# Hyena filters: last layer, decay and spectra issued behind the first tiles of the input projection, and GpSimd's arithmetic of that stage given to VectorE

## The chip, the core and the metric

The kernel runs on one core of a Trainium2 chip. The core has TensorE (matrix products, written to PSUM), VectorE and ScalarE (elementwise work; ScalarE also evaluates functions), GpSimd (elementwise work, without PSUM) and SyncE, from which this kernel issues nearly all of its transfers. Each engine runs its own instructions in order and waits on semaphores of the others. The profile calls them PE (and PEld for its weight loads), DVE, ACT, POOL and SP. The metric is the device time of one execution in microseconds, the median of several.

## The reference, cut to what matters

A diffusion trunk of two layers, on 512 latent and 128 context tokens. Layer 0 mixes with an mLSTM and with a Hyena long convolution, behind one input projection. What the change touches:

```python
hp = rmsnorm(x, g_mix) * (1.0 + sc) + sh        # sc, sh = two of the six columns of silu(c) @ w_ada + b
proj = h @ w_in                                 # 28 column tiles of 128, 12 of them for Hyena
v_h, x1, x2 = split(dwconv3(hy, w_conv_hy))
u = x1 * v_h

def hyena_filters(L, w1, b1, w2, b2, w3, freq):
    hdn = sin(fr * (z @ w1 + b1))
    hdn = sin(fr * (hdn @ w2 + b2))
    filt = hdn @ w3                             # 64 -> 1024
    filt = filt * exp(-t * deltas)              # the decay
    return filt[:, :512], filt[:, 512:]         # h_past, h_future

y_h = x2 * (long_conv_bidir(u, h_past, h_future) + hy_bias * u)   # by spectra of u and of the filters
```

## The kernel before, in words

All tokens lie side by side in 640 columns, with the 1024 features in 8 blocks (k) of 128 partitions. A product in full precision is made of three fp32r matmuls: each operand is split into a high and a low part (`XH`, `XL` for the activations, `hya0h`, `hya0l` and so on for a weight tile), and high*high, high*low and low*high are added in PSUM. ScalarE makes the high part of a weight (L102), another engine the low part (L103, `split_w`).

The start of the program, in `mixer_ab`, is this:

- `hyena_filters` is a generator that the caller steps with `next(filt)`, so that its pieces are issued between others. It loads `z`, `w1`, `w2`, runs the two small sine layers (`fm`, `arg`, `kk`), makes sum and difference of the halves of `w3` and splits them (`fws`, `fwA`, `fwB`), makes five decay blocks with Exp (`ad`), multiplies (`ff`, 20 matmuls of 512 columns, and 10 products `ad<-ff,ad` on VectorE), halves row 0 of two blocks (`row`), and turns the filters into spectra `Ksp`, `Kpp` with cosine and sine tables (`fa`, `fb`, `fp`, 14 matmuls of 512 columns in full fp32).
- `rms` sums the squares of x for the two halves of the columns (`accn`, `sqn`), takes them across partitions on TensorE (`rbn`), and broadcasts 1/rms back (`dgn`, `rbn`).
- `ada_pe` computes shift and scale of four k blocks at a time from 8 weight tiles of 512 KB (`wa`, 16 matmuls `ada`, turned to columns as `adasb`, `adaq`, `mod`, `coefA`). It is called for two halves (k 0 to 3, k 4 to 7), which share 8 buffers.
- `norm_part` then makes for each k and column range `nt` (VectorE), `XH` (ScalarE) and `XL` (VectorE): 12 of each for a half.
- `linear` computes the projection. Its head takes two weight tiles (`hya0`, `hya1`, PSUM `phya`) together, ordered by column half and k so that it can begin before all of x is normalized; each later tile (`hya2`, `hya3`, `hyb4` and on) is 48 matmuls of 320 columns. Behind each tile `done_h` runs the 3-tap convolution (`conv3`, L358 and L361), which frees the tile's PSUM pair, and `filler` steps the filter generator. The head holds both PSUM pairs.
- `front(j)` and `back(j)` are the two parts of the convolution of one block of 128 channels; a written list sets their order among the later tiles.

The order of instructions on each engine isn't that of the source alone: the tile framework's scheduler places what is ready earlier, by its own estimates, and the result is fixed when the program is built. PSUM has two pairs of banks (`pmt`, `pm`) and four single banks (`pst`, `ps`).

Of the kernel before, what the change touches and what calls it, by code (L numbers as in the profile page):

```python
# [36 lines left out]
def trunk(ctx: ExitStack, tc: tile.TileContext, I, O, dbg=None, stop=None):  # L37
# [19 lines left out]
    def pmt(nm):  # L57
        return psum["m"].tile([P, 2, 512], F32, tag="pm", name=nm)

    def pst(nm):  # L60
        return psum["s"].tile([P, 512], F32, tag="ps", name=nm)
# [32 lines left out]
    def load_raw(src, nm):  # L94
        raw = wp.tile([P, 1024], F32, tag="raw", name=nm, bufs=4)
        sp.dma_start(out=raw, in_=src)
        return raw
# [270 lines left out]
    class ConvBufs:  # L368
# [7 lines left out]
        def next(self):  # L376
            self.i += 1
            return self.b[(self.i - 1) % len(self.b)]
# [259 lines left out]
    def hyena_filters(fl, spectra):  # L638

        z = fl.tile([P, 640], F32, name="zt")  # L640
        w1 = fl.tile([P, 64], F32, name="fw1")
        w2 = fl.tile([P, 64], F32, name="fw2")
        fb = fl.tile([64, 4], F32, name="fb")
        arg_ = [fl.tile([64, 640], F32, tag="arg", name=f"arg{j}", bufs=1) for j in range(2)]
        kk = fl.tile([64, 640], F32, tag="kk", name="kk", bufs=1)
        ws = fl.tile([P, 2, 512], F32, name="fws")
        wA = fl.tile([P, 2, 512], F32R, name="fwA")
        wB = fl.tile([P, 2, 512], F32R, name="fwB")
        delta = fl.tile([P, 512], F32, name="delta")
        tneg = fl.tile([P, 5], F32, name="tneg")  # L650
        neg = fl.tile([P, 2, P], F32, name="neg")
        for t_, n_ in ((z, "k_z"), (w1, "w_f1"), (fb, "f_cols"), (w2, "w_f2")):
            sp.dma_start(out=t_, in_=I[n_])
        yield
        w3 = load_raw(I["w_f3"], "fw3")
        for t_, n_ in ((delta, "k_delta"), (tneg, "k_tneg")):
            sp.dma_start(out=t_, in_=I[n_])

        ad = fl.tile([P, 2, 5, 512], F32, name="ad")
        frb = fl.tile([64, 2], F32, name="frb")  # L660
        for j in range(2):
            dve.tensor_tensor(out=frb[:, j : j + 1], in0=fb[:, 0:1], in1=fb[:, 1 + j : 2 + j], op=ALU.mult)
        hid = z
        for j, w in enumerate((w1, w2)):
            pp = pmt(f"fm{j}")
            pt = [pp[:, 0], pp[:, 1]]
            pe.matmul(pt[0][0:64, :], w, hid[:, 0:512], start=True, stop=True)
            pe.matmul(pt[1][0:64, 0:128], w, hid[:, 512:640], start=True, stop=True)
            arg = arg_[j]
            for (c0, c1, a) in ((0, 512, 0), (512, 640, 1)):  # L670
                act.activation(out=arg[:, c0:c1], in_=pt[a][0:64, : c1 - c0], func=AF.Identity,
                               scale=fb[:, 0:1], bias=frb[:, j : j + 1])
            MAGIC = 12582912.0
            dve.tensor_scalar(out=kk, in0=arg, scalar1=1.0 / (2 * math.pi), scalar2=MAGIC, op0=ALU.mult, op1=ALU.add)
            dve.tensor_scalar(out=kk, in0=kk, scalar1=MAGIC, scalar2=None, op0=ALU.subtract)
            c1_ = 6.28125
            c2_ = float(np.float32(2 * math.pi - c1_))
            dve.scalar_tensor_tensor(out=arg, in0=kk, scalar=-c1_, in1=arg, op0=ALU.mult, op1=ALU.add)
            dve.scalar_tensor_tensor(out=arg, in0=kk, scalar=-c2_, in1=arg, op0=ALU.mult, op1=ALU.add)
            lim = 3.14159250  # L680
            dve.tensor_scalar(out=arg, in0=arg, scalar1=lim, scalar2=-lim, op0=ALU.min, op1=ALU.max)
            act.activation(out=hid[0:64, :], in_=arg, func=AF.Sin)
            if j == 0:

                for c, op in enumerate((ALU.add, ALU.subtract)):
                    pool.tensor_tensor(out=ws[:, c], in0=w3[:, 0:512], in1=w3[:, 512:], op=op)
                act.copy(out=wA, in_=ws)
                dve.tensor_tensor(out=wB[0:64], in0=ws[0:64], in1=wA[0:64].bitcast(F32), op=ALU.subtract)
                pool.memset(wB[64:].bitcast(F32), 0.0)

        hs = fl.tile([P, 640], F32R, tag="kk", name="hs", bufs=1)
        act.copy(out=hs[0:64], in_=hid[0:64])
        dve.tensor_tensor(out=hs[64:], in0=hid[0:64], in1=hs[0:64].bitcast(F32), op=ALU.subtract)
        for r in range(5):
            act.activation(out=ad[:, 0, r], in_=delta, func=AF.Exp, scale=tneg[:, r : r + 1])
        yield
        for r in range(5):
            pp = pmt(f"ff{r}")
            pt = [pp[:, 0], pp[:, 1]]
            lh = hs[:, r:512:4] if r < 4 else hs[:, 512:640]  # L700
            for j in range(2):
                pe.matmul(pt[j], lh, wA[:, j], start=True, stop=False)
                pe.matmul(pt[j], lh, wB[:, j], start=False, stop=True)
            for j in (1, 0):
                dve.tensor_tensor(out=ad[:, j, r], in0=pt[j], in1=ad[:, 0, r], op=ALU.mult)
            if r in (0, 4):

                row = fl.tile([64, 640], F32, tag="arg", name=f"row{r}", bufs=1)[0:1, 0:512]
                pool.tensor_tensor(out=row, in0=ad[0:1, 0, r], in1=ad[0:1, 1, r], op=ALU.add)
                for j in range(2):  # L710
                    pool.tensor_scalar(out=ad[0:1, j, r], in0=row, scalar1=0.5, scalar2=None, op0=ALU.mult)
        yield
        Ksp, Kpp, tabs = spectra
        for t_, n_ in ((tabs, "k_tabs"), (neg, "k_neg")):
            sp.dma_start(out=t_, in_=I[n_])
        for cs in range(2):
            src = ad[:, cs]
            p1 = [pst(f"fa{cs}{j}") for j in range(2)]
            pe.matmul(p1[0], tabs[:, 0, cs], src[:, 0], start=True, stop=True)
            pe.matmul(p1[1], tabs[:, 2, cs], src[:, 2], start=True, stop=True)  # L720
            p2 = [pst(f"fb{cs}{j}") for j in range(2)]
            pe.matmul(p2[0], tabs[:, 1, cs], src[:, 1], start=True, stop=False)
            pe.matmul(p2[0], tabs[:, 3, cs], src[:, 3], start=False, stop=True)
            pe.matmul(p2[1], tabs[:, 1, 1 - cs], src[:, 1], start=True, stop=False)
            pe.matmul(p2[1], neg[:, 1 - cs], src[:, 3], start=False, stop=True)
            tt = fl.tile([P, 3, 512], F32, tag="ftt", name=f"ftt{cs}", bufs=1)
            act.copy(out=tt[:, 0], in_=p1[1])
            dve.tensor_tensor(out=tt[:, 1], in0=p1[0], in1=tt[:, 0], op=ALU.add)
            dve.tensor_tensor(out=tt[:, 2], in0=p1[0], in1=tt[:, 0], op=ALU.subtract)

            def c4(ap):
                return ap.rearrange("p (j c) -> p j c", j=4)

            for g in range(4):
                op = ALU.add if g in ((0, 2) if cs == 0 else (0, 3)) else ALU.subtract
                dve.tensor_tensor(out=Ksp[:, :, cs, g], in0=c4(tt[:, 1 + g // 2]), in1=c4(p2[g // 2]), op=op)
            p3 = pst(f"fp{cs}")
            pe.matmul(p3, tabs[:, 4, cs], src[:, 4], start=True, stop=True)
            dve.tensor_copy(out=Kpp[:, :, cs], in_=c4(p3))
        yield  # L740


    def mixer_ab():
        with ExitStack() as es:
# [10 lines left out]
            def W(*idx):  # L755
                return [I["w_ab"][i] for i in idx]
# [17 lines left out]
            with ExitStack() as en:  # L774
# [14 lines left out]
                for half in range(2):  # L789
                    for _ in ada_pe(0, ((0, half), (1, half)), a0, "adr", 8):  # L790
                        pass
                    if half == 0:
                        next(filt)
                    for a in range(2):
                        norm_part(0, 0, nrm, a, rbs[a], range(4 * half, 4 * half + 4))
                    if half == 0:
                        pre = [load_w(w_, f"hya{j}", eng=pool) for j, w_ in enumerate(W(0, 1))]
                es_a.close()
                hy = es_h.enter_context(tc.tile_pool(name="hy", bufs=1, side="right", reuse_waits="tile"))
                tabs = hy.tile([P, 5, 2, P], F32, name="tabs")  # L800
# [118 lines left out]
            def hyb_tile(i):  # L919
                linear(W(i), lambda _, pt, a: done_h(i, pt, a), f"hyb{i}", head=0, filler=filler)  # L920

            for op, j in ((front, 0), (hyb_tile, 4), (hyb_tile, 5), (back, 0), (front, 1), (hyb_tile, 6),
                          (hyb_tile, 7), (back, 1), (qk_tile, 0), (front, 2), (qk_tile, 1), (qk_tile, 4), (back, 2),
                          (qk_tile, 7), (front, 3), (qk_tile, 5), (qk_tile, 3), (qk_tile, 2), (qk_tile, 6),
                          (back, 3)):
                op(j)
# [700 lines left out]
```

## Time and profile before

| | us |
|---|---|
| median of three runs | 1704.24 (1703.04 to 1704.4) |
| the profiled execution | 1707.02 |
| span of its instructions | 1705.2 |
| TensorE busy in the span | 1644.9 (96%) |
| VectorE / ScalarE / GpSimd busy | 1188.9 / 732.4 / 141.8 |
| TensorE takes up the first matmul of the projection | at 48.97 |
| its two-tile head is done | at 70.14 |

The table is of one execution; a busy TensorE has overlapping matmuls, so its share says only that it is hardly ever empty. Times in the rows are from the start of the span.

### The profile page before, as it was taken

Reading aid. Unit: us, or ns where it says so; the run is one execution under the profiler, and the core shown is the slowest. Engines: PE = TensorE matmul, PEld = TensorE weight load, DVE = VectorE, ACT = ScalarE, POOL = GpSimd, SP = SyncE. Lnnn points to the kernel's source line nnn. Section 1 sums busy time; section 2 is a strip of 40 time slices with the busy share of each in tenths; the row PEclk is TensorE's granted clock in tenths of the full one; section 3 lists DMA queues with packets and bytes.
Section 4 is the critical chain, followed back from the end, with each engine's and each line's share of the span. In section 5 each row is a group of like instructions: output and inputs, shape, how many; then the busy total and the mean of one; then the engine's idle time right before and its main releaser. Section 6 shows DMA issues by size and latency. Waiting matters only on the chain. (4 is left out here: it accounts for less than half of the span.)

```text
span 1705.2 us, 28246 instructions
## 1 busy us (share of the span) xinstructions
PE 1644.9 (96%) x11206; PEld 1563.0 (92%) x11206; DVE 1188.9 (70%) x2376; ACT 732.4 (43%) x1385; POOL 141.8 (8%) x153
## 2 busy tenths in 40 slices
PE   5999999999999999999997999999999999999996
PEld 2699888999999999999997899888999999999996
DVE  5887556666887677777467555556389679587785
ACT  6333346663433123223235555656275335244353
POOL 3110001001000000000022212121010000000001
PEclk9999999999999999999999999999999999999998
DMA  8335422142364444454222122211112223222321
GB/s 328 111 125 177 156 76 68 52 147 70 101 184 151 152 148 148 144 173 133 71 96 84 53 60 60 62 47 42 62 50 69 77 79 85 89 75 71 91 79 70
DMA packets 58276, 175.63 MB, mean 103 GB/s; under 512 B 7760, under 2 KB 15232, under 8 KB 57888
## 3 DMA queue, kind: packets, MB, share of 16 engines
q1 hardware_dynamic: 57952, 173.66, 32.5%
q8 instruction: 88, 1.44, 0.3%
q14 instruction: 44, 0.36, 0.1%
q0 software_dynamic: 192, 0.17, 0.1%
HBM read 169.61 MB, written 4.20 MB: 102 GB/s over the span
## 5 line engine op out<-in xcount | busy, mean ns | idle before, releaser
L339 DVE SCALAR_TENSOR_TENSOR x<-pd,mod,x 128x320 f32<-128x320 f32 (+2 forms) x168 | 64.1, 434 | 126.4 <-PE pd L127 120.5
L252 DVE CUSTOM_DVE_ANT_0 adj<-adw,cb 128x1024 f32<-128x1024 f32 x112 | 136.6, 1220 | 1.7 <-DMA adw<-in_w_adaT 0.2
L1324 DVE CUSTOM_DVE_ANT_0 s<-pS,bm 128x384 f32<-128x384 f32 x64 | 34.5, 553 | 30.2 <-PE pS L1323 29.2
L361 DVE SCALAR_TENSOR_TENSOR fcb<-pu,cwf,fcb 128x384 f32<-128x384 f32 (+1 forms) x100 | 53.9, 547 | 1.9
L406 DVE TENSOR_TENSOR pr<-pu,ge 128x384 f32<-128x384 f32 (+1 forms) x42 | 18.7, 485 | 50.1 <-PE pu L127 49.2
L1223 ACT ACTIVATE s<-s,nm 128x384 f32<-128x384 f32 x64 | 39.2, 612 | 20.3 <-DVE nm L1324 18.2
L1225 DVE TENSOR_SCALAR s<-s,nm 128x384 f32<-128x384 f32 (+1 forms) x80 | 46.3, 585 | 1.8
L314 ACT ACTIVATE XH<-nt,mod 128x192 fp32r<-128x192 f32 (+1 forms) x72 | 29.7, 467 | 35.7 <-DVE nt L310 35.6
L1338 ACT COPY pTs<-pS 128x384 f32<-128x384 f32 (+1 forms) x80 | 33.8, 435 | 23.5 <-PE pS L1336 23.1
L1398 POOL TENSOR_TENSOR fo<-fo,rs 128x320 f32<-128x320 f32 x8 | 6.6, 860 | 441.2 <-ACT rs L1390 441.2
L1336 PE MATMUL pS<-ident,s 128*128 128x128 f32 x208 | 36.2, 281 | 5.8 <-DVE s L1225 5.8
L103 POOL TENSOR_TENSOR qk00l<-qk,qk00h 128x1024 fp32r<-128x1024 f32 x1 | 2.8, 2763 | 461.6 <-DVE rn L293 461.6
L278 ACT ACTIVATE sqn<-x 128x320 f32<-128x320 f32 x56 | 25.3, 465 | 36.6 <-DVE x L339 32.6
L1298 POOL TENSOR_TENSOR bm<-amask,wr 128x768 f32<-128x768 f32 x16 | 30.6, 1918 | 113.1 <-issue 84.2
L339 DVE SCALAR_TENSOR_TENSOR x<-pop,mod,x 128x320 f32<-128x320 f32 (+2 forms) x36 | 14.3, 432 | 36.7 <-PE pop L127 26.0
L396 ACT ACTIVATE ge<-fcb 128x641 f32<-128x641 f32 x22 | 16.3, 742 | 52.0 <-DVE fcb L361 52.0
L1316 PE MATMUL pS<-k,q 128*128 128x256 f32 x128 | 31.0, 328 | 7.6 <-DVE k L1251 7.1
L315 DVE SCALAR_TENSOR_TENSOR XL<-nt,mod,XH 128x192 fp32r<-128x192 f32 (+1 forms) x72 | 35.0, 523 | 4.2 <-ACT XH L314 4.2
L604 DVE SCALAR_TENSOR_TENSOR fcb<-fca,cwf,fcb 128x641 f32<-128x641 f32 x38 | 33.5, 883 | 3.5 <-ACT fcb L602 3.2
L1336 PEld LDWEIGHTS pS<-ident,s 128*128 128x128 f32 x208 | 23.6, 141 | 11.6 <-DVE s L1225 9.8
L279 DVE TENSOR_TENSOR accn<-accn,sqn 128x320 f32<-128x320 f32 x56 | 28.9, 522 | 7.2 <-ACT sqn L278 6.2
L127 PE MATMUL pd<-G,d_0h 128*128 128x320 f32 x176 | 33.2, 309 | 0.0
(2125 smaller groups left out, 5875.0 us busy)
## 6 DMA issues: line engine op xcount, KB each, us to landing
adw<-in_w_adaT SPq DMA_DIRECT2D x56, 512.0 KB, 3.8
u<-in_w_up SPq DMA_DIRECT2D x50, 512.0 KB, 3.6
wa<-in_w_ada SPq DMA_DIRECT2D x40, 512.0 KB, 4.9
qk<-in_w_qkv SPq DMA_DIRECT2D x24, 512.0 KB, 3.5
d<-in_w_down SPq DMA_DIRECT2D x16, 448.0 KB, 3.3
d<-in_w_down SPq DMA_DIRECT2D x16, 384.0 KB, 3.1
d<-in_w_down SPq DMA_DIRECT2D x16, 320.0 KB, 2.9
qk<-in_w_ab SPq DMA_DIRECT2D x8, 512.0 KB, 3.7
```

The costliest lines, as they stand in the source:

```text
L127: pe.matmul(bank(pt, a)[:, : sp_[a][1] - sp_[a][0]], ww[:, kt], xx[:, slice(*sp_[a])], start=(first and n == 0), stop=(last and n == 2))
L252: dve.tensor_tensor_reduce(out=jk, in0=w, in1=cb[:, s], op0=ALU.mult, op1=ALU.add, scale=1.0, scalar=0.0, accum_out=acc[:, k, s : s + 1])
L315: last = dve.scalar_tensor_tensor(out=ol, in0=t, scalar=b, in1=oh.bitcast(F32), op0=ALU.add, op1=ALU.subtract)
L339: r = dve.scalar_tensor_tensor(out=x[:, k, c0:c1], in0=bank(pt, h)[:, c0 - h * HT : c1 - h * HT], scalar=mod[:, l, ch, k, s : s + 1], in1= ...
L361: dve.scalar_tensor_tensor(out=o, in0=i, scalar=w[j], in1=o, op0=ALU.mult, op1=ALU.add)
L604: dve.scalar_tensor_tensor(out=o, in0=av[:, d : d + T + 1], scalar=w[j], in1=o, op0=ALU.mult, op1=ALU.add)
L1223: act.activation(out=s, in_=src, func=AF.Exp, scale=-1.0, bias=nm, accum_out=sm)
L1225: dve.tensor_scalar(out=s, in0=s, scalar1=sm, scalar2=None, op0=ALU.mult)
L1316: pe.matmul(pS[:, 0:256], qq, kk[b][e][:, i * P : i * P + 256], start=(kk is k1), stop=(kk is k2))
L1324: dve.tensor_tensor_reduce(out=s, in0=pS[:, 0:384], in1=bm[e][:, (0, 1, 1, 2)[i]], op0=ALU.add, op1=ALU.min, scale=1.0, scalar=3.0e38, acc ...
L1336: pe.transpose(pS[:, j * P : (j + 1) * P], s[:, j * P : (j + 1) * P], ident)
L1338: act.copy(out=t[:, : nk * P], in_=pS[:, : nk * P])
```

## The change

The filter generator stops behind the two sine layers. What follows in it (load of `w3`, `delta` and `tneg`, `fws`, `fwA`, `fwB`, the decay, `ff`, the spectra) is issued by the fillers behind the head and behind the third and fourth tile; `ff` takes the single banks in place of the pairs. GpSimd's arithmetic of the stage (`fws`, the row halving, the low parts of `hya0` and `hya1`) goes to VectorE. `hyb4` is issued ahead of `front(0)`, and `hyb6` and `qk0` each ahead of a `back`.

```diff
@@ hyena_filters
         yield
-        w3 = load_raw(I["w_f3"], "fw3")
-        for t_, n_ in ((delta, "k_delta"), (tneg, "k_tneg")):
-            sp.dma_start(out=t_, in_=I[n_])
-
-        ad = fl.tile([P, 2, 5, 512], F32, name="ad")
...
-            if j == 0:
-
-                for c, op in enumerate((ALU.add, ALU.subtract)):
-                    pool.tensor_tensor(out=ws[:, c], in0=w3[:, 0:512], in1=w3[:, 512:], op=op)
-                act.copy(out=wA, in_=ws)
-                dve.tensor_tensor(out=wB[0:64], in0=ws[0:64], in1=wA[0:64].bitcast(F32), op=ALU.subtract)
-                pool.memset(wB[64:].bitcast(F32), 0.0)
...
         dve.tensor_tensor(out=hs[64:], in0=hid[0:64], in1=hs[0:64].bitcast(F32), op=ALU.subtract)
+        yield
+        w3 = load_raw(I["w_f3"], "fw3")
+        for t_, n_ in ((delta, "k_delta"), (tneg, "k_tneg")):
+            sp.dma_start(out=t_, in_=I[n_])
+
+        ad = fl.tile([P, 2, 5, 512], F32, name="ad")
+
+        for c, op in enumerate((ALU.add, ALU.subtract)):
+            dve.tensor_tensor(out=ws[:, c], in0=w3[:, 0:512], in1=w3[:, 512:], op=op)
+        act.copy(out=wA, in_=ws)
+        dve.tensor_tensor(out=wB[0:64], in0=ws[0:64], in1=wA[0:64].bitcast(F32), op=ALU.subtract)
+        pool.memset(wB[64:].bitcast(F32), 0.0)
         for r in range(5):
             act.activation(out=ad[:, 0, r], in_=delta, func=AF.Exp, scale=tneg[:, r : r + 1])
-        yield
         for r in range(5):
-            pp = pmt(f"ff{r}")
-            pt = [pp[:, 0], pp[:, 1]]
+            if r == 2:
+                yield
+                yield
+            pt = [pst(f"ff{r}{j}") for j in range(2)]
...
-                pool.tensor_tensor(out=row, in0=ad[0:1, 0, r], in1=ad[0:1, 1, r], op=ALU.add)
+                dve.tensor_tensor(out=row, in0=ad[0:1, 0, r], in1=ad[0:1, 1, r], op=ALU.add)
                 for j in range(2):
-                    pool.tensor_scalar(out=ad[0:1, j, r], in0=row, scalar1=0.5, scalar2=None, op0=ALU.mult)
+                    dve.tensor_scalar(out=ad[0:1, j, r], in0=row, scalar1=0.5, scalar2=None, op0=ALU.mult)
@@ mixer_ab
-                    if half == 0:
-                        next(filt)
...
-                        pre = [load_w(w_, f"hya{j}", eng=pool) for j, w_ in enumerate(W(0, 1))]
+                        pre = [load_w(w_, f"hya{j}") for j, w_ in enumerate(W(0, 1))]
...
-            for op, j in ((front, 0), (hyb_tile, 4), (hyb_tile, 5), (back, 0), (front, 1), (hyb_tile, 6),
-                          (hyb_tile, 7), (back, 1), (qk_tile, 0), (front, 2), (qk_tile, 1), (qk_tile, 4), (back, 2),
+            for op, j in ((hyb_tile, 4), (front, 0), (hyb_tile, 5), (hyb_tile, 6), (back, 0), (front, 1),
+                          (hyb_tile, 7), (qk_tile, 0), (back, 1), (front, 2), (qk_tile, 1), (qk_tile, 4), (back, 2),
```

What the scheduler makes of it, at three places. First, VectorE in the changed kernel, at the end of the first half of the normalization; `hya0l` and `hya1l` are the low parts of the head's two weight tiles, `mod` and `coefA` begin the second half:

```order
L310 SCALAR_TENSOR_TENSOR nt_320_332<-x,coefA,rbn_201 128x192
L315 SCALAR_TENSOR_TENSOR XL<-nt_320_324,mod,XH 128x192
L315 SCALAR_TENSOR_TENSOR XL<-nt_512_328,mod,XH 128x128
L315 SCALAR_TENSOR_TENSOR XL<-nt_320_332,mod,XH 128x192
L310 SCALAR_TENSOR_TENSOR nt_512_336<-x,coefA,rbn_201 128x128
L103 TENSOR_TENSOR hya0l<-hya_340,hya0h 128x1024
L315 SCALAR_TENSOR_TENSOR XL<-nt_512_336,mod,XH 128x128
L103 TENSOR_TENSOR hya1l<-hya_346,hya1h 128x1024
L235 TENSOR_TENSOR mod<-adaq_387,bada 128x8 x2
L208 SCALAR_TENSOR_TENSOR coefA<-mod,gains 128x8
```

The two low parts, which stood on GpSimd, now stand behind 23 (`hya0l`) and all (`hya1l`) of the 24 instructions of the first half of the normalization. Second, TensorE in the changed kernel at the beginning of the head; `ada_352` is the second half's product with the `wa` tiles, `phya` the head:

```order
L224 MATMUL ada_352<-wa_361,csil 32x512
L224 MATMUL ada_352<-wa_362,csil 32x512
L224 MATMUL ada_352<-wa_369,csil 32x512
L121 MATMUL phya_451<-XH,hya0l 128x320
L121 MATMUL phya_451<-XL,hya0h 128x320
...
L224 MATMUL ada_352<-wa_370,csil 32x512
L224 MATMUL ada_352<-wa_369,csil 32x512
L224 MATMUL ada_352<-wa_370,csil 32x512
...
L121 MATMUL phya_452<-XH,hya1l 128x320
...
L224 MATMUL ada_352<-wa_377,csil 32x512
```

Two head matmuls and nine of the sixteen `ada` matmuls come ahead of the first that reads `hya0l`; the other seven stand behind it, in three groups, with 20 head matmuls between. Third, TensorE behind the head, before and in the changed kernel; `ff` are the filters' last layer, `fb`, `fp` and `fa` the spectra, and `phya_671` and `phya_604` the third tile:

```order
L121 MATMUL phya_510<-XL,hya1h 128x320
L723 MATMUL fb_627<-ad,tabs 128x512
L724 MATMUL fb_628<-ad,tabs 128x512
L725 MATMUL fb_628<-ad,neg 128x512
L738 MATMUL fp_641<-ad,tabs 128x512
L719 MATMUL fa_644<-ad,tabs 128x512
L720 MATMUL fa_645<-ad,tabs 128x512
L127 MATMUL phya_671<-XH,hya2h 128x320 x2
```

```order
L121 MATMUL phya_452<-XL,hya1h 128x320
L703 MATMUL ff_578<-fwA,hs 128x512
...
L703 MATMUL ff_591<-fwA,hs 128x512
L704 MATMUL ff_578<-fwB,hs 128x512
...
L704 MATMUL ff_591<-fwB,hs 128x512
L127 MATMUL phya_604<-XH,hya2h 128x320 x2
```

Where six spectra matmuls stood between head and third tile, there are now eight matmuls of `ff`, which read `fwA` and `fwB`. Behind the first tiles of the query and key projection the order of every engine is the same in both kernels.

## Rows read from the trace of the kernel before

**Rows 1.** The page: TensorE's busy tenths in 40 slices of 42.6 us.

```profile
PE   5999999999999999999997999999999999999996
```

**Rows 2.** Windows: stretch, length, busy PE, PEld, DVE, ACT, POOL; PEclk, DMA, GB/s.

```profile
59.28:68.79 9.51, 9.51 (x55) 8.07 (x54) 8.81 (x26) 5.30 (x13) 0.00 (x0) 1.00 0.55 209
48.97:70.14 21.17, 21.17 (x128) 16.63 (x125) 18.20 (x52) 11.21 (x27) 4.32 (x3) 1.00 0.38 138
70.14:103.77 33.63, 33.63 (x193) 28.01 (x191) 27.21 (x47) 9.06 (x17) 1.83 (x1) 1.00 0.36 114
101.00:103.77 2.77, 2.77 (x20) 2.58 (x18) 2.77 (x5) 0.18 (x1) 1.83 (x1) 1.00 0.00 0
```

**Rows 3.** Timeline of the start: start, length, engine, instruction [idle before].

```profile
14.37 4.68 DVE L279 TENSOR_TENSOR accn<-accn,sqn 128x320 f32<-128x320 f32 x5 [0.17 <-ACT sqn L278]
15.15 2.96 POOL L686 TENSOR_TENSOR fws<-fw 128x512 f32<-128x512 f32 x2 [9.24 <-DMA fw<-in_w_f]
26.29 4.45 PE L224 MATMUL ada<-wa,csil 128*32 128x512 f32 x22
31.56 1.90 PE L224 MATMUL ada<-wa,csil 128*32 128x512 f32 x10
35.54 0.56 ACT L229 COPY adasb<-ada 128x512 f32<-128x512 f32 x1
38.14 0.24 DVE L235 TENSOR_TENSOR mod<-adaq,bada 128x8 f32<-128x8 f32 x2 [0.79 <-PE adaq L232]
40.66 0.54 DVE L310 SCALAR_TENSOR_TENSOR nt<-x,coefA,rbn 128x320 f32<-128x320 f32 x1
```

**Rows 4.** Groups by line on DVE, 14.3 to 18.4 us, then 18.9 to 25 us.

```profile
L279 DVE TENSOR_TENSOR accn<-accn,sqn 128x320 f32<-128x320 f32 x4 | 3.9, 987 | 0.4 <-ACT sqn L278 0.2
...
L279 DVE TENSOR_TENSOR accn<-accn,sqn 128x320 f32<-128x320 f32 x6 | 2.9, 488 | 0.3
```

**Rows 5.** Timeline of SP's queue: the second eight `wa` transfers.

```profile
28.26 5.75 SPq L220 DMA_DIRECT2D wa<-in_w_ada  x8
```

**Rows 6.** Timeline of the head of the projection.

```profile
37.12 2.37 POOL L103 TENSOR_TENSOR hya0l<-hya,hya0h 128x1024 fp32r<-128x1024 f32 x1 [19.02 <-ACT hya0h L102]
48.97 0.41 PE L118 MATMUL phya<-XH,hya0h 128*128 128x320 f32 x1
49.90 1.06 PE L224 MATMUL ada<-wa,csil 128*32 128x512 f32 x6
50.88 0.41 PE L121 MATMUL phya<-XL,hya0h 128*128 128x320 f32 x1
59.28 1.46 DVE L310 SCALAR_TENSOR_TENSOR nt<-x,coefA,rbn 128x320 f32<-128x320 f32 x3
```

**Rows 7.** Windows of half a microsecond, columns as in rows 2.

```profile
33.50:34.00 0.50, 0.00 (x0) 0.00 (x0) 0.00 (x0) 0.50 (x2) 0.00 (x0) 1.00 0.84 287
...
36.50:37.00 0.50, 0.50 (x5) 0.50 (x3) 0.34 (x1) 0.50 (x2) 0.00 (x0) 0.52 1.00 402
...
43.00:43.50 0.50, 0.50 (x3) 0.17 (x1) 0.00 (x0) 0.00 (x0) 0.50 (x2) 0.65 0.17 66
```

**Rows 8.** Timeline: two `ff` matmuls, and what stands behind the head.

```profile
45.31 0.40 PE L702 MATMUL ff<-fwA,hs 128*128 128x512 f32 x1
...
45.55 0.39 PE L703 MATMUL ff<-fwB,hs 128*128 128x512 f32 x1
...
69.90 1.21 DVE L103 TENSOR_TENSOR hya2l<-hya,hya2h 128x1024 fp32r<-128x1024 f32 x1
69.94 1.04 ACT L102 CAST hya3h<-hya 128x1024 fp32r<-128x1024 f32 x1
71.00 1.02 PE L724 MATMUL fb<-ad,tabs 128*128 128x512 f32 x2
71.86 1.02 PE L725 MATMUL fb<-ad,neg 128*128 128x512 f32 x2
73.51 1.92 DVE L361 SCALAR_TENSOR_TENSOR abc<-phya,cwh,abc 128x384 f32<-128x384 f32 x4
```

## The prediction

> **What bounds the kernel now.** I read the page's slices first: the reader is to see that TensorE is short of work in the first slice alone, apart from one later dip [rows 1]. Then the windows: from the first matmul of the projection's head at 48.97 to the end of tile `hyb4` at 103.77 it is busy in every microsecond, 21.17 of 21.17 and 33.63 of 33.63, with VectorE busy 18.20 and 27.21 beside it [rows 2]. So there is little idle time for moved work to fill behind 49 us, and time can only be won ahead of it; what makes TensorE wait later is lost. All orders agree behind the stage, and I expect a shift won or lost there to stay to the end. I measure it at one point: the head, the tiles `hya2`, `hya3`, `hyb4` and all filter work done, without `front(0)`. Before, that is 103.77 less the front's 2.77 of TensorE time [rows 2], 101.0.
>
> **The start gains 6.7 us.** VectorE's sums of squares take 987 ns each beside GpSimd's `fws` and 488 ns a little later, alone [rows 4]; five of them last 4.68 us around the 2.96 us of `fws` [rows 3]. Without `fws` that is up to 2.0 us; I take 1.9, as ScalarE's squares then feed them just in time. The other bound is nothing, if ScalarE holds them. The Trainium skill, "SBUF — State Buffer", section "Who interferes with whom", says that a VectorE instruction with two SBUF inputs and a GpSimd one that reads SBUF exclude each other for a whole instruction. By that rule up to 2.96 us would come free; the row's doubling agrees in kind, and the sum goes by the row.
>
> The first `ada` product ends at 31.56 + 1.90 = 33.46, after standing still for the broadcast of the second 1/rms [rows 3]. With the 1.9, and 0.7 for the decay's activations and table loads that leave ScalarE ahead of the second square root, it ends at 30.9. `adasb` then starts at 31.0 instead of 35.54, since no decay activation is queued ahead of it on ScalarE. `mod` follows 2.6 us later (35.54 to 38.14 [rows 3]), 33.6, and the first `nt` at 34.0 instead of 40.66; the `ad` products that stood between are gone. SP's queue loses 0.77 MB (`w3`, `delta`, `tneg`) ahead of the `wa` tiles, 1.9 us at the 402 GB/s of [rows 7]. That is hidden: the first eight were there when wanted, and the second eight are issued at 28.26 [rows 5], when the first matmuls free their buffers, so they come with the 1.9 above and have landed by about 37.
>
> **Then TensorE stands still for `hya0l`.** GpSimd had it done at 37.12 + 2.37 = 39.5 [rows 6]. VectorE now makes it behind 23 of the 24 normalization instructions. The second half's 24, without GpSimd beside them, took 9.51 us [rows 2]; the last `XL` is 0.35 of it. A low part costs 1.21 [rows 8]. So `hya0l` is done at 34.0 + 9.16 + 1.21 = 44.4. TensorE does two head matmuls and nine of the sixteen `ada` of the second half by 39 and waits, with everything behind that in its queue. Seven `ada` are among them, and without these VectorE has no second `mod`: both engines wait for each other's work in turn.
>
> From 44.4, 20 head matmuls and three `ada` groups come first. A group costs 0.98 (49.90 to 50.88 [rows 6]). Head matmuls cost 0.15: of the 21.17 us [rows 2], three spectra matmuls at 0.86 [rows 8], three `ada` groups and 1.0 for `adaq` leave 14.7 for 96. That is 3.0 + 2.9 = 5.9. From there to the first `nt` are 2.4, as `adasb` to `mod` above without the lower clock, plus the coefficient.
>
> **The clock.** Before, TensorE ran dry at 33.5, and from about 36.5 to 43.3 the granted clock was 0.5, the 1.2 GHz level, back at 2.4 only after TensorE had worked through several microseconds of it [rows 7]. Here it is empty for over 5 us. The same stretch of 6.8 us behind 44.4 would cost half of itself, 3.4; none costs nothing. I take 2.5, near the row. The Trainium skill, "TensorE: Matmul & The Clock Gate", section "HAM oscillation — how this bites in real kernels", says that waits between bursts of matmuls bring the half rate back each time, so that a stop is paid twice. The rows agree as far as one stop shows it; it speaks against this change.
>
> So the second half's first `nt` is at 44.4 + 5.9 + 2.5 + 2.4 = 55.2, against 59.28 [rows 6]. Its 9.5 us carry two `fws` more on VectorE; for 512 columns I take half of 1.21, 1.2 for both (bounds: nothing, 2.4). With 0.5 for the last matmuls the head ends at 66.4, against 70.14: **3.7 won.** That is all that is left of 6.7.
>
> **Behind the head 12.8 are lost.** Before, three of the 14 spectra matmuls and all 20 `ff` were done by then, the `ff` in a stretch where TensorE waited anyway. Now they run where it is the bound: 3 at 0.86 (71.00 to 71.86) and 20 at 0.23 (45.31 to 45.55 [rows 8]) are 2.6 + 4.6 = 7.2. The ten `ad` products and five Exp go along and stay hidden beside TensorE, save in the waits that follow.
>
> New waits are 5.6. The first `ff` needs `fwA`, which ScalarE casts behind its last `XH` and `hya2h`, two casts of 1.04 [rows 8]: it is there 0.9 behind the head's end. `fwB` comes behind `hya2l` on VectorE, two times 1.21, with four `ff` in between: 0.5. The third tile needs a PSUM pair. The head holds both, and `conv3` of both tiles is interleaved behind `fwB`: seven steps at 0.48 (four in 1.92 [rows 8]) are 3.4, with 0.9 of `ff` to cover them: 2.5. Before, six spectra matmuls, 5.2 us, lay over this. Later `ff` and spectra share four single banks and wait for VectorE, which has the row halving (six short steps, under 0.6 each) in its way: I take 1.7. Together the bounds are 2.9 (the first three partly covered) and 7.5.
>
> **The sum** is 66.4 + (33.63 - 2.77) + 7.2 + 5.6 = 110.1, against 101.0: 9.1 longer. Against the profiled execution's 1707.02 that is 1716.1; the median of the runs is 2.8 lower, 1704.24, and gives **1713.3**. With the clock at 0 to 3.4 and perhaps once more behind the head, waits at 2.9 to 7.5, and the sums' gain at 0 to 1.9, this case reaches from 1708 to 1720.
>
> **The rivals.**
> *Faster, 1702.* TensorE doesn't wait for `hya0l`: VectorE is through with the first half long before. Then the seven `ada` are done by 43, the second half begins when VectorE is free, at 43.9, the clock stays up, and the sum falls by 11.3 to 2.2 under before. It decides at the second `nt`: 46.1 is break-even. For it: the weights have landed and GpSimd no longer slows VectorE. Against it: the instruction order, and 24 steps that took 9.51.
> *Same, 1705.* The waits behind the head are covered and the clock doesn't fall: 9.1 - 5.6 - 2.5 = 1.0 over before. For it: both are bounds rather than rows. Against it: the PSUM pairs, which the order shows to be taken.
> *Slower still, 1718.* The clock falls twice, at `hya0l` and again in the waits behind the head: 0.9 + 3.4 more.
>
> **How the numbers follow.** The likeliest case has 0.61, slower still 0.11, same 0.12, faster 0.16. A change of 0.2%, 3.4 us, is about what a measurement of this kernel tells from none. Slower by more than that: 0.71, with nearly all of the first two; same 0.13; faster 0.16. The range leaves out the faster case and the top of the slow one: 1703.5 to 1720.
>
> **What would show it.** In the changed kernel's timeline: the first `nt` near 34; `hya0l` on DVE near 43 to 44.5, and PE's first L121 of the head right behind it, with an idle time of 4 us or more that ends on DVE; PEclk at 0.5 for some microseconds around 45; the second `adasb` near 53; the head's end near 66; L127 of the third tile waiting for DVE L361. I am wrong if TensorE takes up the head before 40 without a long stop, or if the later part of the kernel takes the shift back.

## The result, and the profile after

The changed kernel takes 1714.86 us (median of 4 runs, 1714.15 to 1715.15), the kernel before 1704.32 (4 runs, 1703.04 to 1706.67): 1.0055 times as long, 95% interval 1.004 to 1.007. The profiled execution of after took 1714.15, with a span of 1712.4; the one of before was 2.7 above its median, so the spans differ by 7.2 and the medians by 10.5.

The timeline of after, from the start to the second half of the normalization, answers to [rows 3] and [rows 6]:

```profile
28.91 1.92 PE L224 MATMUL ada<-wa,csil 128*32 128x512 f32 x14
30.91 0.59 ACT L229 COPY adasb<-ada 128x512 f32<-128x512 f32 x1 [2.67 <-PE ada L224]
33.42 1.47 DVE L310 SCALAR_TENSOR_TENSOR nt<-x,coefA,rbn 128x320 f32<-128x320 f32 x3 [0.34 <-DVE coefA L208]
36.58 4.71 PE L224 MATMUL ada<-wa,csil 128*32 128x512 f32 x18
41.71 1.22 DVE L103 TENSOR_TENSOR hya0l<-hya,hya0h 128x1024 fp32r<-128x1024 f32 x1
42.99 0.41 PE L121 MATMUL phya<-XH,hya0l 128*128 128x320 f32 x1 [1.70 <-DVE hya0l L103]
43.92 1.06 PE L224 MATMUL ada<-wa,csil 128*32 128x512 f32 x6
46.56 1.05 PE L224 MATMUL ada<-wa,csil 128*32 128x512 f32 x2
48.46 1.06 PE L224 MATMUL ada<-wa,csil 128*32 128x512 f32 x6
49.63 0.59 ACT L229 COPY adasb<-ada 128x512 f32<-128x512 f32 x1 [7.39 <-PE ada L224]
51.36 0.24 DVE L235 TENSOR_TENSOR mod<-adaq,bada 128x8 f32<-128x8 f32 x2 [7.03 <-PE adaq L232]
51.84 1.47 DVE L310 SCALAR_TENSOR_TENSOR nt<-x,coefA,rbn 128x320 f32<-128x320 f32 x3
62.30 0.31 PE L121 MATMUL phya<-XL,hya1h 128*128 128x320 f32 x1
```

The first `nt` is 7.2 us sooner than in [rows 3]. TensorE then waits 1.70 for `hya0l`, and VectorE stands 7.03 for the second `adaq`: the mutual wait. The head ends at 62.5, against 70.14 in [rows 2].

Behind the head, and later in the kernel, the timeline has four waits of TensorE that before had not, or had shorter, and one group of `ada` in two pieces:

```profile
63.34 1.33 PE L703 MATMUL ff<-fwA,hs 128*128 128x512 f32 x4 [0.73 <-ACT fwA L691]
64.87 1.30 PE L704 MATMUL ff<-fwB,hs 128*128 128x512 f32 x4 [0.20 <-DVE fwB L692]
68.15 0.87 PE L127 MATMUL phya<-XH,hya2h 128*128 128x320 f32 x2 [1.98 <-DVE abc L361]
...
106.04 1.04 PE L224 MATMUL ada<-wa,csil 128*32 128x512 f32 x2
107.01 0.75 PE L833 MATMUL ut<-ident,x 128*128 128x128 f32 x4
107.60 0.27 PE L834 MATMUL up<-ident,x 128*128 128x128 f32 x1
107.80 1.06 PE L224 MATMUL ada<-wa,csil 128*32 128x512 f32 x6
...
379.47 0.53 PE L127 MATMUL pop<-XH,op00h 128*128 128x320 f32 x2 [1.48 <-DVE x L339]
```

The windows of after, columns as in [rows 2], show where the clock fell: ahead of the long run of head matmuls (33.5 to 40.5, while TensorE was starved and then did `ada`), not in that run, which begins at 43, and again behind it:

```profile
33.50:40.50 7.00, 5.12 (x19) 1.53 (x20) 7.00 (x20) 4.79 (x11) 0.00 (x0) 0.52 1.03 411
43.00:62.50 19.50, 19.24 (x116) 15.12 (x116) 11.77 (x32) 10.64 (x21) 0.00 (x0) 1.00 0.39 131
62.50:105.65 43.15, 40.24 (x193) 32.64 (x193) 33.31 (x56) 9.59 (x16) 0.00 (x0) 0.96 0.33 100
66.30:68.10 1.80, 0.00 (x0) 0.00 (x0) 1.80 (x5) 0.54 (x1) 0.00 (x0) 0.93 0.21 87
68.10:71.50 3.40, 3.35 (x13) 3.38 (x14) 3.40 (x7) 0.00 (x0) 0.00 (x0) 0.53 0.02 5
```

At the prediction's point (end of `hyb4`, `front(0)` not counted) after stands at 105.65 and before at 103.77 - 2.77 = 101.0, so after is 4.7 behind. At the first matmul of tile `qk4` it is 6.4 behind, at the matmul `pop` 7.4. The matmuls of `front(0)` in before, between 93.66 and 97.88, and the first of `qk4` in before and in after:

```profile
93.66 0.63 PE L834 MATMUL ut<-ident,x 128*128 128x128 f32 x4
95.62 2.05 PE L844 MATMUL hc<-uts,tabs 128*128 128x128 f32 x16
97.51 0.61 PE L875 MATMUL hq<-uts,tabs 128*128 128x128 f32 x4
...
157.31 0.56 PE L127 MATMUL pqk<-XH,qk40h 128*128 128x320 f32 x2
...
163.68 0.56 PE L127 MATMUL pqk<-XH,qk40h 128*128 128x320 f32 x2
```

### The profile page after: what moved, and what is told of

The parts are those of the page before. It is cut to its first block, busy times and chain, and to the rows that moved or that the text cites. A ratio compares the mean times of both kernels' runs of the same rounds, so it can differ in the third digit from the quotient of the medians.

```text
span 1712.4 us, 28238 instructions
## 1 busy us (share of the span) xinstructions
PE 1646.7 (96%) x11206; PEld 1564.1 (91%) x11206; DVE 1190.4 (70%) x2386; ACT 727.9 (43%) x1382; POOL 126.5 (7%) x143
## 5 line engine op out<-in xcount | busy, mean ns | idle before, releaser
L1337 ACT COPY pTs<-pS 128x384 f32<-128x384 f32 (+1 forms) x80 | 33.8, 435 | 23.7 <-PE pS L1335 23.4
L127 PE MATMUL pd<-G,d_1h 128*128 128x320 f32 x176 | 33.1, 309 | 0.0
```

The source lines that it names most:

```text
L127: pe.matmul(bank(pt, a)[:, : sp_[a][1] - sp_[a][0]], ww[:, kt], xx[:, slice(*sp_[a])], start=(first and n == 0), stop=(last and n == 2))
```

## The experiments

**The kernel before, profiled again.**

> The kernel before, unchanged, for a second profile. The profiled executions differ by 7.2 us in span (1705.2 and 1712.4), the medians by 10.5. First theory: the first profile of before was a long execution, and this one has a span of 1701 to 1703, with the same head (start 49.0, end 70.1) and the difference spread over later places, mostly where the granted clock falls. Rival: the difference is in the stage itself, and the head of this execution starts or ends 2 to 3 us sooner, at 46 to 47 or 67 to 68.

It took 1702.63, with a span of 1700.9. Its windows:

```profile
33.50:44.00 10.50, 9.82 (x37) 5.67 (x36) 8.42 (x13) 4.69 (x7) 7.24 (x4) 1.00 0.84 326
45.85:67.03 21.18, 21.18 (x129) 16.65 (x126) 18.49 (x53) 11.20 (x27) 4.38 (x4) 1.00 0.38 138
67.03:100.56 33.53, 33.53 (x193) 28.02 (x191) 27.11 (x47) 8.96 (x17) 1.74 (x1) 1.00 0.38 114
```

The rival held, for 3.1 of the 4.3 us: the same instructions in the same order, but the clock never left 1.0 where [rows 7] has it at 0.5 from 36.5 to 43.3. The head starts at 45.85 instead of 48.97, with the same length (21.18, 21.17); 0.4 of this was there before the clock fell, at the first `ff`. TensorE's stop ahead of that `ff` was not the same, since in `e0` the first `ada` product ended 0.8 later. The row of the first execution, then that of `e0`:

```profile
35.30 0.62 PE L702 MATMUL ff<-fwA,hs 128*128 128x512 f32 x1 [1.84 <-DVE hs L693]
...
34.94 0.62 PE L702 MATMUL ff<-fwA,hs 128*128 128x512 f32 x1 [0.66 <-DVE hs L693]
```

After a stop of 1.84 us the clock fell, after one of 0.66 it did not. The other 1.2 us come near 900 us, where the first profile had a granted clock of 0.91 for 20 us and this one 1.00. The median of before lies between its two profiles. In this execution the point is at 100.56 - 2.77 = 97.8, so after is 7.9 behind at the point, and 11.5 at the end.

**The engine part alone: `e1`.** Before, with

```diff
-                    pool.tensor_tensor(out=ws[:, c], in0=w3[:, 0:512], in1=w3[:, 512:], op=op)
+                    dve.tensor_tensor(out=ws[:, c], in0=w3[:, 0:512], in1=w3[:, 512:], op=op)
...
-                        pre = [load_w(w_, f"hya{j}", eng=pool) for j, w_ in enumerate(W(0, 1))]
+                        pre = [load_w(w_, f"hya{j}") for j, w_ in enumerate(W(0, 1))]
```

and the row halving likewise.

> The kernel before with the stage's GpSimd arithmetic (fws, the halved rows, hya0l and hya1l) on VectorE, and nothing moved. First theory, that the placement of the filter work costs the time: the start gains at most 1.9 us (the sums of squares no longer at 987 ns), VectorE takes 2 x 0.68 for fws, six short row steps and 2 x 1.22 for the low parts, 5 us in all, of which its idle time ahead of the first nt hides about half: 1703 to 1707, within 0.2% of before. Rival, that the change of engine costs the time: most of the 10.5 us appear here too, 1710 or more.

Measured: 1710.03, ratio 1.0030 (1.002 to 1.004), at the foot of the rival. The window of the head, and VectorE's timeline in it:

```profile
48.35:72.20 23.85, 21.51 (x122) 16.61 (x120) 21.83 (x57) 11.93 (x28) 0.00 (x0) 1.00 0.42 144
```
```profile
58.45 1.22 DVE L103 TENSOR_TENSOR hya1l<-hya,hya1h 128x1024 fp32r<-128x1024 f32 x1
60.18 0.23 DVE L235 TENSOR_TENSOR mod<-adaq,bada 128x8 f32<-128x8 f32 x2
61.65 1.47 DVE L310 SCALAR_TENSOR_TENSOR nt<-x,coefA,rbn 128x320 f32<-128x320 f32 x3
```

With the `ad` products still in this stage VectorE is busy 21.83 of the head's 23.85 us, more than TensorE (21.51): the second `mod`, whose `adaq` ended at 53.5, stands behind other VectorE work until 60.18, and the head is 2.7 us longer than before. TensorE waits 2.3 us in it, 1.2 of them for `XH`, which needs VectorE's `nt`, and 0.7 for the transfer of the tables. In the changed kernel, where the decay has been moved away, VectorE is busy only 11.77 of the 19.50 us.

**The low parts elsewhere: `e2` and `e3`.** The changed kernel with `eng=pool` in the line of `pre` (`e2`); the changed kernel with that line ahead of the first half's `norm_part`, on VectorE (`e3`).

> The changed kernel with hya0l and hya1l made on GpSimd again, all else as changed. First theory: the wait for hya0l is worth what the trace shows, 1.7 us, plus the 2.4 us that VectorE spends on the two low parts between the halves; the head ends 2 to 4 us sooner, at 58.5 to 60.5, and the time is 1711 to 1713. Rival, that the low parts set off the mutual waiting in which VectorE stands still for 7.0 us for adaq: that falls to under 3 us, the head ends at 56 to 57, and the time is 1708 to 1710. Second rival: the ada are held by their transfers and by GpSimd slowing VectorE's normalization (steps of two SBUF inputs up from 0.49 to about 0.99 for 4.7 us): no change, 1714 to 1716.

> The changed kernel with the weights hya0 and hya1 loaded and split ahead of the first half of the normalization, on VectorE. VectorE stands still for 3.5 us for the first adaq, and the low parts take 2.4. First theory: they fit in that idle time if the high parts are cast by then; ScalarE casts hya0h at 31.4 behind adasb, so hya0l is done at 33.7 and holds up the first nt by 0.3 to 1.5 us, TensorE has head matmuls from 34.6 on, the wait of 1.7 us is gone, and the ada between the head's matmuls come sooner: head's end 58 to 60, time 1710 to 1713. Rival: nothing but the wait's place changes, because the ada of the second half set the second adaq; VectorE's idle time ahead of the second mod stays at 7 us or more, and the time is 1714 to 1716.

Both theories fell: 1717.94 (ratio 1.0081, 1.0064 to 1.0097) and 1718.09 (1.0079, 1.0064 to 1.0094), some 3 us slower than the changed kernel. TensorE's timeline of `e2`, and windows:

```profile
52.40 1.06 PE L224 MATMUL ada<-wa,csil 128*32 128x512 f32 x8
54.23 1.06 PE L232 MATMUL adaq<-selc,adasb 128*128 128x4 f32 x8 [0.76 <-ACT adasb L229]
56.99 0.41 PE L118 MATMUL phya<-XH,hya0h 128*128 128x320 f32 x1 [1.71 <-ACT XH L314]
```
```profile
53.30:57.00 3.70, 1.23 (x13) 0.98 (x9) 1.61 (x6) 1.21 (x3) 0.00 (x0) 1.00 0.66 213
57.00:60.50 3.50, 3.50 (x14) 3.33 (x15) 3.40 (x9) 3.47 (x6) 0.00 (x0) 0.56 0.92 310
```

With the low parts early, the order on TensorE changed: 48 head matmuls stand ahead of the last `ada` of the second half (in after 22). All that the first half allows is then done by 52.4, the second `adasb` comes at 53.59 (after: 49.63), TensorE stands still for the second half, and the clock falls behind that stop. In the changed kernel the wait for `hya0l` had held head matmuls back and let nine `ada` go first; in `e2`, without it, the head goes on from 36.46 instead of 42.99, and the whole is slower.

**The order of `ada` and head: `e4` to `e7`.** In all four

```diff
-                linear(W(0, 1, 2, 3), done_h, "hya", filler=lambda: next(filt, 0), kcut=4, pre=pre, x_last=True)
+                with tc.issue_after(lastada[0]):
+                    linear(W(0, 1, 2, 3), done_h, "hya", filler=lambda: next(filt, 0), kcut=4, pre=pre, x_last=True)
```

where `lastada[0]` is the second half's last `ada` matmul; `e5` with the low parts of `e3`, `e6` with the loads of `w3`, `delta` and `tneg`, `fws`, `fwA` and `fwB` ahead of the `yield` that the change put before them, `e7` with both.

> The changed kernel with TensorE's matmuls of the projection queued behind the last ada of the second half (an edge of order alone). In e2 and e3 TensorE had head matmuls early, ran them ahead of the ada, and stood still for the second half of the normalization. First theory, that the order of ada and head on TensorE decides how long the head lasts: adasb of the second half starts at 41 to 43 instead of 49.6, VectorE's idle time ahead of the second mod is under 2 us instead of 7.0, and the head ends at 58.5 to 60 because the ada (14 of them stood among the head's matmuls, 2.9 us) are done in time in which TensorE waited; median 1711 to 1713. Rival: TensorE is busy from 43.0 to 62 in the changed kernel anyway, VectorE's idle time costs nothing, and the ada cost the same ahead of the head: head's end 62 to 63, 1714 to 1716.

> As e4, and the low parts ahead of the first half's normalization as in e3. First theory: with the order of e4 the early low parts are worth what the wait for hya0l showed and more: the head starts at 40 to 41.5, right behind the ada, and ends at 56 to 58.5; median 1708 to 1711, 2 to 3 us under e4. Rival, that early low parts harm by themselves (they push VectorE's first half back by 2.4 us, and with it the second): head's end no sooner than in e4, 59 or later, median at or above e4's.

> As e4, and fws, fwA and fwB made where the kernel before loads w_f3, ahead of the normalization; Exp, ff and spectra stay behind. First theory, that the waits behind the head (0.73 for fwA, 0.20 for fwB, 1.98 for the PSUM pair behind conv3) and the fall of the clock at 68 to 71.5 come from fwA and fwB being made late: the first two are gone, the third is 1 us or less, the clock stays at 1.0 there, and the stretch from the head's end to the end of hyb4 is 3 to 5 us shorter than the 43.2 of the changed kernel; the start loses 1 to 2 us to w_f3 and fws. Median 1 to 4 us under e4. Rival: the third tile waits for the pair as long as before (2 us or more), since conv3 of both tiles is what holds it, and the clock falls again: the stretch is shorter by under 1.5 us, median at or above e4's.

> The order of e4, the low parts of e5 and the early w_f3 products of e6 together. First theory, that the three losses add: head's end 57 to 60, head's end to the end of hyb4 39 to 41, median 1704 to 1708, so near the kernel before. Rival: the gains overlap, because what is won ahead of the head is lost as TensorE's idle time and low clock behind it: median no more than 1 us under the best of e4 to e6, 1709 or more.

Measured, with the points of the traces worked out as above:

| kernel | median us | ratio (95%) | head's first L121, end | head's end to `hyb4`'s end |
|---|---|---|---|---|
| after | 1714.86 | 1.0055 (1.004 to 1.007) | 42.99, 62.5 | 43.2 |
| `e4` | 1710.09 | 1.0029 (1.0018 to 1.0040) | 44.29, 61.7 | 41.7 |
| `e5` | 1710.43 | 1.0034 (1.0022 to 1.0046) | 42.94, 59.7 | 42.1 |
| `e6` | 1711.30 | 1.0039 (1.0024 to 1.0054) | 44.62, 62.4 | 40.0 |
| `e7` | 1711.82 | 1.0039 (1.0025 to 1.0053) | 44.12, 64.8 | 40.0 |

That the order is what made `e3` slow is shown by `e5`, which differs from `e3` in the order alone: 1710.43 against 1718.09, 7.7 us. Against the changed kernel the order is worth 4.8 us of the medians in `e4`, more than either theory said. The two traces show 2.2 of it by `qk4` (161.43 against 163.68) and 3.8 at the end; 1.4 of that comes near 900 us, where the two executions of before differ too, so how much of the 4.8 the order itself made is not shown. The head of `e4` ends only 0.7 sooner: the three groups of `ada` are out of it, 2.9 us, but it starts 1.3 later, and behind new stops for `hya0l` and `hya1l` the clock is at 0.57 from 46 to 50. The stretch behind it is 1.5 shorter, for `fwA` and `fwB` are made ahead of the head's end, and TensorE waits for neither:

```profile
57.94 1.04 ACT L693 CAST fwA<-fws 128x1024 fp32r<-128x1024 f32 x1
59.21 1.21 DVE L694 TENSOR_TENSOR fwB<-fws,fwA 64x1024 fp32r<-64x1024 f32 x1
```

In `e6` these two waits are gone as well, and from the head's end on the clock stays up:

```profile
62.40:102.43 40.03, 38.57 (x194) 31.09 (x193) 30.75 (x54) 7.15 (x12) 0.00 (x0) 1.00 0.29 83
```

That is 3.2 us off the changed kernel's 43.2, within what the first theory said, and only the wait for the PSUM pair is left, at 1.46, more than it said. `e4` has the same wait, 1.45; what `e6` has over it, 1.7 us, is the clock, which in `e4` stands at 0.5 for some 3 us there. Why it stayed up in `e6` is not shown, since `fwA` and `fwB` were early in both. The first `nt` of `e6` is at 35.39, in `e4` at 34.73; that `w_f3` ahead of `wa` cost this is argued only, for single profiles with one and the same start differ by more (`e9` below). In `e5` TensorE waits 1.17 for the second `adasb`, with a low clock just ahead of it; its head ends 2 us before that of `e4`, but not at 56 to 58.5. Neither has a median under that of `e4`. In `e7` TensorE waits 2.47 for the second `adasb` and the clock falls behind it:

```profile
44.50:47.50 3.00, 0.53 (x5) 0.27 (x3) 2.47 (x9) 2.22 (x7) 0.00 (x0) 1.00 0.80 257
48.00:54.50 6.50, 6.50 (x26) 6.50 (x27) 5.59 (x16) 3.22 (x8) 0.00 (x0) 0.50 0.68 248
```

So the gains don't add: the rival of `e7` held. All four stay 5.9 to 7.6 us above before.

**The move without the engines, and the list: `e8`, `e9`.** `e8` is the changed kernel with `fws`, row halving and low parts on GpSimd again, `e9` the changed kernel with the list of operations of before.

> The changed kernel with all of the stage's arithmetic on GpSimd as before, so the move and the new list alone. With the low parts on GpSimd the order on TensorE puts head matmuls ahead of the ada again, as in e2. First theory, that this order and the moved filter work set the time: as e2, second adasb at 52 to 54, TensorE empty for 3 to 5 us ahead of the second half's matmuls and the clock at 0.5 behind it, median 1716 to 1719, slower than the changed kernel; the engine part of the change then does not add to the move. Rival, that the two parts add: the engine part alone cost 5.6 us in e1, so without it the changed kernel's 10.5 falls to 5 and the median is 1708 to 1711.

> The changed kernel with the list of operations behind the projection as before (front 0 ahead of hyb4). First theory: the list costs and brings nothing by itself, since TensorE is busy there in both orders: median 1714 to 1716, and the shift against before at the end of qk1 within 1 us of the changed kernel's 6.4. Rival: front 0 right behind the last spectra product waits for Ksp (four combines on VectorE) or for conv3 of hya3: TensorE waits 1 us or more there, 1716 to 1718; or it covers a wait of the changed kernel's order, 1712 to 1713.

`e8`: 1714.95, ratio 1.007 (1.0051 to 1.0088), the time of the changed kernel, so the engine part adds nothing on top of the move, though alone it cost 5.5. The trace is that of the first theory (second `adasb` at 53.49, stop, low clock), and the time lies 1 us under what that theory gave. `e9`: 1711.79, ratio 1.0043 (1.0028 to 1.0058). Up to the head's end its order is that of the changed kernel on every engine, yet this execution has its first `nt` at 34.99 instead of 33.42 and ends its head 1.5 later: so much do single profiles of one order differ there. From the head's end to `qk4` it takes 163.89 - 64.0 = 99.9, after 163.68 - 62.45 = 101.2. Nearly 1.0 of these 1.3 us is the group of `ada` that the new list lets `front(0)` cut in two; here it is whole:

```profile
110.34 1.07 PE L224 MATMUL ada<-wa,csil 128*32 128x512 f32 x8
```

The medians differ by more, 3.1, with intervals that overlap; the rest isn't settled.

**Towards a better version: `e10`, `e11`.** Before with only `fws` on VectorE (`e10`); that with the order of `e4` (`e11`).

> The kernel before with only fws on VectorE. The sums of squares no longer run beside it (987 against 488 ns), and VectorE takes 2 x 0.68 for fws. First theory: of the start's gain this part is worth 0.5 to 1.5 us: first nt at 38.3 to 39.5 against 39.7 and 40.7 in the two profiles of before; TensorE fills what is ahead of the head with ff as before, and the median is 1702.5 to 1704. Rival: the head's start hangs on the ff and ada that stand ahead of it in TensorE's order, not on nt: median 1704 to 1706.

> As e10, with the projection's matmuls queued behind the last ada of the second half, as in e4. First theory: the order that was worth 4.8 us in e4 is worth something here too, 0.5 to 2 us, as second adasb comes sooner and VectorE does not wait for the second mod: median 1701 to 1703. Rival: in this kernel TensorE is busy from 35 us on with ff, ada and head, so the order is worth nothing, or costs the time in which TensorE waits for wa: median 1704 to 1707.

`e10`: 1707.06, ratio 1.0013 (1.0004 to 1.0022). The first `nt` is at 38.29, as expected, but `ff` and `ada` are ordered otherwise, one `ff` waits 1.23 for an `ad` product, and the head starts at 48.25. `e11`: 1705.24, ratio 1.0005 (0.9995 to 1.0014), the same as before. No version beat the kernel before.

## Why the prediction was right, and where its steps were not

**The bound and the start: right.** First `ada` product at 30.83 (predicted 30.9), `adasb` 30.91 (31.0), first `nt` 33.42 (34.0). In the profiles of `e2`, `e3`, `e4`, `e5`, `e8` and `e9` the first `nt` stands at 33.8 to 35.0, and in the two of before at 39.7 and 40.7. What a GpSimd instruction does to VectorE's is seen in `e2`, where `coefA`, eight elements wide, took 2.02 us instead of 0.17:

```profile
32.77 2.02 DVE L208 SCALAR_TENSOR_TENSOR coefA<-mod,gains 128x8 f32<-128x8 f32 x1
```
```profile
32.44 2.33 POOL L103 TENSOR_TENSOR hya0l<-hya,hya0h 128x1024 fp32r<-128x1024 f32 x1 [26.56 <-ACT hya0h L102]
```

It ends with `hya0l` at 34.8. The Trainium skill, "SBUF — State Buffer", section "Who interferes with whom", says that a VectorE instruction with two SBUF inputs and a GpSimd one that reads SBUF exclude each other for a whole instruction; these rows agree with it better than the doubling of [rows 4] did.

**The wait for `hya0l`: right in place and cause, too large.** `hya0l` was done at 42.9 (predicted 44.4, as the first half took 8.3 ahead of it and not 9.16), and the nine `ada`, expected done by 39, ran to 41.3 at half clock. So 1.70 was left of over 5. The second eight `wa`, taken to be there by about 37, came later: in `e4`, which asks for them in a row, TensorE waits four times for one, the last time at 41:

```profile
40.98 1.06 PE L226 MATMUL ada<-wa,csil 128*32 128x512 f32 x6 [0.28 <-DMA wa<-in_w_ada]
```

The seven `ada` among the head's matmuls and the mutual wait came as said.

**The clock term of 2.5 stood in the wrong place.** It fell between 33 and 34, while TensorE stood empty, and was back between 40 and 41; the head ran at 1.0 throughout. There it cost nothing that shows: the nine `ada` done at half clock ended 1.70 ahead of `hya0l`. The second half began at 51.84 (55.2): 2.5 sooner by the clock and 1.5 by `hya0l`, while the `ada` groups and the second `mod` took 0.5 more than predicted. The head ended at 62.5 (66.4). This is the step that failed: 3.7 won by the head's end was 7.7 in the two profiles, 4.5 against `e0`. The fall came behind the head instead, at 68.1 to 71.5, where 3.35 busy us at 0.53 cost an estimated 1.6. The rival "slower still" had a second fall there, and it happened without the first. The break-even of the faster rival, a second half from 46.1 on, was not reached.

**Behind the head: 12.8 predicted, 12.3 measured** (43.15 against 33.63 - 2.77 = 30.9), with other parts. The 2.77 of the front is right, but the row that the prediction names for it, 101.00 to 103.77, shows tile `hyb4`; the front's matmuls are those at 93.66 to 97.88 above. The moved work is 7.2 by count. The three waits were 0.73, 0.20 and 1.98 (predicted 0.9, 0.5 and 2.5); the 1.7 for later `ff` and spectra didn't come; the clock's 1.6 did. Some 0.6 us is left that I can't assign. `e4` shows that the waits for `fwA` and `fwB` go when these are made early, and that the third becomes 1.45; `e6` shows 3.2 us less where the clock stays up too. That the rest is the moved work itself was not shown by a run of its own: the best stretch, 40.0, is 9 us above that of before, and the count's 7.2 with the one wait of 1.46 make 8.7 of it.

**That the shift stays to the end: nearly.** It grew from 4.7 to 6.4 by `qk4`, nearly 1.0 of it by the cut group of `ada`, which no term had, the rest in small pieces that I can't assign. And it grew by 1.05 at `pop`, where TensorE waits 1.5 for a PSUM buffer instead of 0.4. The waits of `e0`, then of after, 160 to 400 us (in total, times, longest):

```profile
PE pop L127 <- DVE x L339: 0.4, 1, 0.4
```
```profile
PE pop L127 <- DVE x L339: 1.5, 1, 1.5
```

All nine kernels with `ff` in single banks have the 1.5, and before and all three with `ff` in pairs the 0.4. That five `ff` pairs less turn the rotation of the two pairs, so that `pop` gets the buffer that is released last, is argued only.

**The sum** was 9.1 at the point. The profiles gave 4.7, about half, and 7.9 against the other execution of before. By the medians it is 10.5 at the end, and the changed kernel's 1714.86 is 1.6 over the predicted 1713.3. The verdict rests on the trade that the prediction named: the start wins less than the filter's work costs where TensorE is the bound. That the sum came so near is in good part luck, by errors that cancel: the gain by the head's end was put 4 us too small against the profile that the prediction used, the later losses of 2.8 were missing, and that profile of before was a long one.

## What to carry to other kernels

Work that another engine does while TensorE is short of work is cheap there; moving it behind the point at which TensorE is the bound costs its length there, here 7.2 us by count, whatever the start wins. When a wait is taken away, print the order again: here `e2` and `e3` removed a wait, and the scheduler put head matmuls ahead of the `ada` that everything else waited for. Take a second profile of the kernel before, before a stop or a low clock in one profile becomes a term: two profiles of one order differed by 3.1 us at the head's end of before, and by 1.5 at that of the changed kernel and `e9`.

## What the runs showed of the hardware

At a granted clock of 1.0 a lone `ada` matmul of 32 columns (two records, x2) takes 1.04 us, three (x6) 1.06 and four (x8) 1.07: a group costs the same whole or in part, so each cut costs about 1.0. The Trainium skill, "TensorEngine Tiling (Array Packing)", section "Key Properties", says that tiles of the array can run matmuls in parallel; the rows agree.

The same order of instructions can lose the clock or keep it: in one execution of before TensorE stood empty for 1.84 us, and 1.2 GHz followed from 36.5 to 43.3; in the other it stood empty for 0.66 us at the same place, and ran at 2.4 GHz all through. The heads lie 3.1 us apart, nearly 0.2% of this kernel. But the length of a stop doesn't tell the outcome alone: behind the same wait of some 1.46 us for the third tile's PSUM pair the clock was at 0.5 for some 3 us in `e4` and `e5`, and at 1.0 in `e6` and `e7`. The rule of the Trainium skill on which the prediction drew ("TensorE: Matmul & The Clock Gate", "HAM oscillation — how this bites in real kernels") agrees with the stops of after, `e2` and `e7`; behind the PSUM wait of `e6` and `e7` no low clock followed.
